# Other places in VectorE's queue for a recurrence's products and updates, an earlier residual load, and later sums of an input norm

## The chip, the cores and the metric

The program runs on one core of a Trainium2 chip. The core has five engines with a queue each: TensorE (PE in the profile, its weight loads PEld), VectorE (DVE), ScalarE (ACT), GpSimd (POOL) and SyncE (SP), which issues all the DMA transfers here. Each queue is worked off in order; semaphores hold an instruction back until the data it needs are there. The metric is the device time of one execution in microseconds (us); lower is better.

## The reference

One inference step of a two-layer decoder: layer 0 is a gated DeltaNet, layer 1 an RWKV-7 time mixing; each is a pre-norm sub-layer with a residual add, and a final norm follows. All data are float32. There are 1104 token columns: 64 sample tokens (8 sequences of 8), 16 meta tokens and 1024 prompt tokens.

```python
def rwkv_mixer(xn, S0, shift_prev, ...):
    xx = xprev - xn
    xs = xn[None] + xx[None] * mu[:, None, None, :]
    rkvz = jnp.einsum('sbtd,sde->sbte', xs[:4], w_rkvz)      # r, k, v, z
    w = -jax.nn.softplus(-(w0 + jnp.tanh(xs[4] @ w1) @ w2)) - 0.5
    a = jax.nn.sigmoid(a0 + (xs[5] @ a1) @ a2)
    kk = l2norm((k * k_k).reshape(B, T, H, N))
    k = k * (1.0 + (a - 1.0) * k_a)
    decay = jnp.exp(-jnp.exp(w))
    def step(S, inp):                                        # per token
        S = (S * d_t[:, :, None, :]
             + jnp.einsum('bhvk,bhk->bhv', S, -kk_t)[..., None] * b_t[:, :, None, :]
             + v_t[..., None] * k_t[:, :, None, :])
        return S, jnp.einsum('bhvk,bhk->bhv', S, r_t)
    ...
    y = (y - mean) * lax.rsqrt(var + GN_EPS) * lnx_w + lnx_b # per head
    y = y + jnp.sum(r_h * k_h * r_k, -1, keepdims=True) * v_h # the bonus
    y = y.reshape(B, T, D) * jax.nn.silu(z)
    return y @ w_o, S, xn[:, -1]

x = x + gdn_mixer(rmsnorm(x, norm_w[0]));  x = x + rwkv_mixer(rmsnorm(x, norm_w[1]))
y = rmsnorm(x, final_norm_w)
```

Outputs are the normed rows of prompt and sample, and the states of both layers.

## The kernel before

Activations lie feature-major: a tile has 128 features on the partitions and columns of tokens. The columns are worked in three thirds (`SEGS`: 384, 384 and 336 columns). Dense products keep float32 precision with three passes over split operands: a high part rounded to fp32r (made by ScalarE, instructions at L139: whi, yh, prh) and the remainder (GpSimd or VectorE, L143: wlo, yl, prl).

*Between the layers* (`gdn_out_norm`, L1200): for each third, eight output tiles of the DeltaNet's output projection are computed and added to the residual xb (L1196). After the eighth, `rwkv_norm` (L1246) squares the third on ScalarE, adds the squares on VectorE (rsum, L1260), sums over partitions with matmuls (frss), takes the root, spreads it with further matmuls against a diagonal dg (frb) and scales xb (L1275). The scaled input feeds the low-rank products (dlora). This stretch is not ordered by hand: a planner lists the instructions, and the order of the code gives their priority.

*Projections* (`projections`, L2394): the r, v and z products, ordered by hand in gaps between output tiles. In the same gaps 24 items are prepared (an item is a third times one of eight pairs of heads; `system_steps`, L1567): VectorE forms kk and al from k, a and the decay, TensorE the 64x64 systems (fL), and GpSimd inverts them step by step (L690, L692).

*The recurrence* (`wave`, L2531): rounds tau from -2 to 52. Each item starts at round T = 2n and takes six rounds, one per chunk of 64 columns, so that three items are under way at a time; the state is kept per pair of heads. A round has phases 0 to 3 (and 1.5). In phase 0 `step_solve` makes X from the state (ScalarE, L1891), in phase 1 `step_inner` solves (rA from X and rTT), then `step_state` updates the state (VectorE rS, L1920). Everything else is put into a plan with a round, a phase and a priority, and issued phase by phase in order of priority:

```python
        put = lambda tau, ph, f, prio: plan.setdefault((tau, ph), []).append((prio, f))

        def emit(*at):
            for _, f in sorted(plan.pop(at, []), key=lambda x: x[0]):
                f()
```

So the order in every engine's queue, SyncE's included, is the order of the plan. The steps that matter here, for an item at T:

- loads at T-5 and T-4 (cs, r, k2, al, v, kp);
- `reads` (L1738: r times decay, the two-input product AR) at T-3 and `pair` (L1742: pr, the bonus product of r, k and r_k), then `halves` (prh on ScalarE, prl on GpSimd);
- `bonus` (L1748) at T-2: matmuls fbonus with prh and prl, and rbv on VectorE; `scores` (G) in phase 1 of T-2 and T-1; `keys` (fBT) at T-1;
- `stats` of the chunk's output in phase 2 of each of its rounds (L1828, L1829);
- `rwkv_finish` (L1922) from T+5 to T+8: root of the variance (GpSimd's power, then three VectorE steps), normalised y (GpSimd, L1944), transposition dyT, t (L1952), the gated output lz (L1954), its split yh, yl (L1959). Items 22 and 23 have plans of their own;
- for the eight items of the first third, the sample sequences: `rwkv_sample_read` loads the states sn, transposes them (dsn) into Sb and reads them (drsr); `rwkv_sample_write` spreads the updates by sequence (ue), multiplies (drsw), adds to Sb (L2006) and decays it (L2007), transposes back (dsbT), copies (sso) and stores with four DMAs.

Filler matmuls run in phases 2 and 3 (`fill`, priorities 2.5 and 1): first the rest of z, then the output projection (`project_out`, L2021: tiles zo, added to the residual x2 at L2041), whose weights come as a stream (wraw, whi, wlo). `finish` (L2059) is the final norm of a third: transposes (fin), squares, times the weight (L2077), root, and the scaling by rows (L2092), which is GpSimd's in the first third. The PSUM tags of this part, with their buffers, are f (2), r (3), d, x and z (1 each), and a buffer is reused when its reader is done.

## Time and profile before

| | us |
|---|---|
| three runs | 2199.70, 2207.82 (median), 2214.87 |
| the profiled execution | 2200.14 |
| its span, first to last instruction | 2198.4 |
| TensorE busy in it | 2083.4 |
| VectorE, ScalarE, GpSimd busy | 1434.5, 1260.2, 1253.1 |

The clock column of a view is the TensorE clock granted, as a share of the full one. Over the whole span it was 0.98. In the rows of a view, an instruction is told by its engine, its line in the kernel, and output<-inputs by name; the first letter of a PSUM tile's name is its tag (drsw is a tile of tag d). "A <- B: total, times, longest" says that A waited for B. In a timeline, a bracket gives the idle time before an instruction and what ended it; a wait for several things is put down to the one that came last by the profile, and where the engine named had long been done it was another, often a DMA.

### The profile page before, as it was taken

To read this page: it belongs to the slowest core of one execution; us is meant where nothing else is said; L and a number is where in the kernel's file an instruction comes from. 1 tells how busy PE (TensorE), PEld (TensorE's weight loads), DVE (VectorE), ACT (ScalarE), POOL (GpSimd) and SP (SyncE) were. 2 spreads that over 40 slices of the span, in tenths; PEclk is the share of its full clock that TensorE was granted. 3 is DMA by queue.
4 is the path that set the end of the run, shared out by engine and by line. 5 is a ranking of instruction groups with operands and counts; after the bars stand their busy time and mean duration, and the time that the engine had idled before them with its cause. 6 is when DMAs were issued, how large, how long until landed. Compare 5 with 4: busy or idle time off the path is not lost. (4 is left out here: it accounts for less than half of the span.)

```text
span 2198.4 us, 56220 instructions
## 1 busy us (share of the span) xinstructions
PE 2083.4 (95%) x20958; PEld 1945.7 (89%) x20958; DVE 1434.5 (65%) x3644; ACT 1260.2 (57%) x3627; POOL 1253.1 (57%) x1896
## 2 busy tenths in 40 slices
PE   7999999999999999989998999999989988899997
PEld 6888989898999989978998999998879977798886
DVE  7868585767757585975434762767756346687765
ACT  6536565656655565645433474755655456677763
POOL 3428577685858585625240452228668736676873
PEclk9999999999999999999999999999999999999998
DMA  3324242424243332436244235587785666566543
GB/s 122 91 75 115 73 133 67 118 78 112 79 113 97 100 111 69 138 79 176 93 140 117 73 93 174 172 257 204 228 241 153 166 179 171 159 186 171 160 124 103
DMA packets 510763, 291.67 MB, mean 133 GB/s; under 512 B 240777, under 2 KB 495866, under 8 KB 510490
## 3 DMA queue, kind: packets, MB, share of 16 engines
q1 hardware_dynamic: 510490, 288.08, 46.6%
q8 instruction: 166, 2.72, 0.5%
q14 instruction: 107, 0.88, 0.1%
HBM read 195.66 MB, written 92.30 MB: 131 GB/s over the span
## 5 line engine op out<-in xcount | busy, mean ns | idle before, releaser
L143 POOL TENSOR_TENSOR wlo<-wraw,whi 128x512 fp32r<-128x512 f32 x190 | 250.7, 1320 | 229.5 <-ACT whi L139 200.4
L692 POOL TENSOR_TENSOR invT<-invT,invtmp 72x31 f32<-72x31 f32 (+36 forms) x341 | 213.4, 626 | 26.7
L634 DVE SCALAR_TENSOR_TENSOR cvy<-raw,cw,cvy 128x408 f32<-128x408 f32 (+2 forms) x288 | 200.4, 696 | 31.1 <-ACT cvy L115 27.0
L690 POOL TENSOR_TENSOR invtmp<-invA,invT 72x31 f32<-72x31 f32 (+36 forms) x341 | 203.8, 598 | 24.9 <-DMA invA<-rltd 5.1
L129 PE MATMUL d<-xc,whi 128*128 128x384 f32 (+1 forms) x640 | 175.7, 339 | 0.2 <-ACT ev L1434 0.2
L139 ACT CAST whi<-wraw 128x512 fp32r<-128x512 f32 x238 | 145.9, 615 | 34.5 <-DMA wraw<-in_rwkv_w_o 12.4
L129 PE MATMUL dv<-xc,whi 128*128 128x384 f32 (+1 forms) x480 | 154.2, 342 | 0.0
L129 PE MATMUL dz<-xc,whi 128*128 128x384 f32 (+1 forms) x480 | 152.2, 340 | 0.0
L115 ACT ACTIVATE w<-rA,nbp 128x128 f32<-128x128 f32 x144 | 45.1, 364 | 152.5 <-PE rA L129 150.1
L1944 POOL TENSOR_SCALAR y<-y,mv,grs 128x64 f32<-128x64 f32 x132 | 83.7, 651 | 66.5 <-DVE grs L164 53.3
L129 PEld LDWEIGHTS d<-xc,whi 128*128 128x128 f32 x640 | 117.0, 190 | 2.2 <-ACT ev L1434 0.5
L129 PE MATMUL d<-xc,wlo 128*128 128x384 f32 (+1 forms) x320 | 104.2, 335 | 2.1 <-DVE wlo L143 2.1
L160 POOL TENSOR_TENSOR ors<-ovar,cvals 128x6 f32<-128x6 f32 x24 | 34.1, 1422 | 125.0 <-DVE ovar L1122 125.0
L129 PE MATMUL dz<-xa,whi 128*128 128x384 f32 (+1 forms) x288 | 102.6, 356 | 0.5 <-DVE zg L906 0.5
L129 PE MATMUL dv<-xa,whi 128*128 128x384 f32 (+1 forms) x288 | 102.0, 354 | 0.0
L129 PE MATMUL d<-xa,whi 128*128 128x384 f32 (+1 forms) x336 | 95.9, 338 | 1.3 <-POOL xa L143 0.8
L129 PEld LDWEIGHTS dv<-xc,whi 128*128 128x128 f32 x480 | 89.0, 188 | 3.5 <-issue 3.0
L959 POOL TENSOR_SCALAR Sb<-Sb,eglb 128x128 f32<-128x128 f32 x128 | 88.6, 704 | 5.9 <-DVE usc L752 3.1
L129 PEld LDWEIGHTS dz<-xc,whi 128*128 128x128 f32 x480 | 89.9, 190 | 0.6 <-issue 0.2
L129 PE MATMUL d<-xh,whi 128*128 128x384 f32 (+1 forms) x256 | 82.1, 333 | 0.0
L129 PE MATMUL d<-xl,whi 128*128 128x384 f32 (+1 forms) x256 | 82.1, 334 | 0.0
L129 PE MATMUL d<-xh,wlo 128*128 128x384 f32 (+1 forms) x256 | 81.8, 333 | 0.0
(558 smaller groups left out, 7304.3 us busy)
## 6 DMA issues: line engine op xcount, KB each, us to landing
wraw<-in_gdn_w_in SPq DMA_DIRECT2D x96, 256.0 KB
wraw<-in_rwkv_w_rkvz SPq DMA_DIRECT2D x74, 256.0 KB
Sb<-in_state_gdn SPq DMA_DIRECT2D x64, 256.0 KB
wraw<-in_rwkv_w_o SPq DMA_DIRECT2D x48, 256.0 KB
E<-drow SPq DMA_DIRECT2D x24, 384.0 KB
attn<-drow SPq DMA_DIRECT2D x24, 384.0 KB
wraw<-in_gdn_w_out SPq DMA_DIRECT2D x36, 256.0 KB
out_s_gdn<-Sb SPq DMA_DIRECT2D x32, 256.0 KB
```

The lines of the kernel that those rows point to most:

```text
L115: return self.nc.scalar.activation(out, in_, func, bias=bias, scale=scale, **kw)
L129: self.nc.tensor.matmul(out, lhsT, rhs, start=start, stop=stop)
L139: nc.scalar.copy(hi, x)
L143: e.tensor_tensor(lo, x, hi.bitcast(F32), op=ALU.subtract)
L160: self.nc.gpsimd.tensor_tensor(y, x, half.broadcast_to(sh), op=ALU.pow)
L634: nc.vector.scalar_tensor_tensor(ys[s][:, 0:wd(s)], raws[s][:, k:k + wd(s)], cw[k], ys[s][:, 0:wd(s)], op0=ALU.mult, op1=ALU.add)
L690: v.tensor_tensor(tmp, A[:, j, j + 1:32].unsqueeze(2).broadcast_to([nb, n, m]), Tv[:, j, 0:m].unsqueeze(1).broadcast_to([nb, n, m]), op=AL ...
L692: v.tensor_tensor(Tv[:, j + 1:32, 0:m], Tv[:, j + 1:32, 0:m], tmp, op=ALU.subtract)
L959: nc.gpsimd.tensor_scalar(Sb[g][:, u], Sb[g][:, u], self.eglb[:, hv, 4 * g + u:4 * g + u + 1], None, op0=ALU.mult)
L1944: nc.gpsimd.tensor_scalar(y[:, q], y[:, q], mv[:, q, 0:1], P.rs[:, q:q + 1], op0=ALU.subtract, op1=ALU.mult)
```

## The change

Seven edits. (1) `rwkv_norm` becomes a generator: its squares follow the third as before, its sums come in the code after the second output tile of the next third, and the spreading after the third tile; the last third's follow at once. dg gets a third buffer. (2) Two memsets per item in `system_steps` go from GpSimd to VectorE. (3) In the recurrence, `reads` and `pair` go to the head of phase 2 of round T-3 (priorities -1.5 and -1.2, from 3.5 and from phase 3), `halves` to 2.95 there. (4) The sample read's transposes go from phase 3 to phase 2 (2.9); the sample write's add goes to -0.5, its decay becomes a step of its own at 3, the transposes back go to 2.4, and the four stores follow in two pairs, in phase 3 and at the next round's start. (5) The gated output goes to -2 in phase 2, its split to 2.6; for items 22 and 23 the root's VectorE steps go from phase 0 to phase 2. (6) The first three tiles of the residual are loaded from round 14 + 16 s, phase 3, and the further ones one tile earlier than before. (7) The final norm's row scaling in the first third goes from GpSimd to VectorE, and the second third's norm steps from priority 2.45 to 2.55, behind the filler.

```diff
--- before.py
+++ after.py
@@ -1218,12 +1218,17 @@
                 elif s == 0:
                     self.load_w(src(ft), into=w)
                 self.add_out(s, self.dense(w, 128, oh, ol, s, bufs=4), xb[ft], self.x1T[ft])
+                if s and ft in (1, 2):
+                    next(norm, None)
                 if s == 2 and ft == 1:
                     lw = self.lora_weights(flat(xa)[:, 0:2048], flat(xa)[:, 2048:4096], pool)
             if s == 0:
                 for ft in (0, 1):
                     self.load_w(src(ft), into=res[ft])
-            self.rwkv_norm(s, xb, og, pool)
+            norm = self.rwkv_norm(s, xb, og, pool)
+            next(norm)
+        for _ in norm:
+            pass
         return lw
 
 
@@ -1248,7 +1253,6 @@
         nc, t = self.nc, self.t
         c0, n = SEGS[s]
 
-        ssp = self.ps("f", 2, "rss")
         sum_ = t(lp, [128, 384], "rsum", 1)
         if n < 384:
             nc.gpsimd.memset(sum_[:, n:384], 1.0)
@@ -1258,14 +1262,17 @@
                 self.act(f(sq), d, AF.Square)
             if k:
                 nc.vector.tensor_tensor(sum_[:, 0:n], sum_[:, 0:n], sq[:, 0:n], op=ALU.add)
+        yield
+        ssp = self.ps("f", 2, "rss")
         for q in range(3):
             self.mm(ssp[:, 16 * q:16 * q + 16], sum_[:, 128 * q:128 * q + 128], self.ones[:, 0:16])
         ms, rs = t(lp, [128, 3], "rms", 2), t(lp, [128, 3], "rrs", 2)
         nc.vector.tensor_scalar(ms, ssp[:, 0:48].rearrange("p (q j) -> p q j", j=16)[:, :, 0], 1.0 / D, RMS_EPS, op0=ALU.mult, op1=ALU.add)
         self.rsqrt(rs, ms, lp, "rr")
+        yield
         rb = self.ps("f", 2, "rb")
         for q in range(3):
-            dg = t(lp, [128, 128], "dg", 2)
+            dg = t(lp, [128, 128], "dg", 3)
             nc.vector.tensor_scalar(dg, self.ident, rs[:, q:q + 1], None, op0=ALU.mult)
             self.mm(rb[:, 128 * q:128 * q + 128], self.ones, dg)
         nw = self.pcol["norm_w"]
@@ -1574,9 +1581,9 @@
         kk, iD = t(pool, [128, 384], "skk", 3), cs
         al, sq = t(pool, [128, 384], "sal", 3), t(pool, [128, 384], "sqs", 3)
         self.act(al[:, 1:384], cs[:, 0:383], AF.Exp, scale=-self.DEC)
-        nc.gpsimd.memset(c6(al)[:, :, 0:1], 1.0)
+        nc.vector.memset(c6(al)[:, :, 0:1], 1.0)
         if Q.s == 0:
-            nc.gpsimd.memset(al[:, 0:64].rearrange("p (b r) -> p b r", r=8)[:, :, 0:1], 1.0)
+            nc.vector.memset(al[:, 0:64].rearrange("p (b r) -> p b r", r=8)[:, :, 0:1], 1.0)
         self.act(sq, k, AF.Square, scale=pc("rwkv_k_k"))
         nc.vector.scalar_tensor_tensor(kk, k, pc("rwkv_k_k"), a, op0=ALU.mult, op1=ALU.mult)
         nc.vector.scalar_tensor_tensor(al, k, pc("rwkv_k_k"), al, op0=ALU.mult, op1=ALU.mult)
@@ -1797,10 +1804,10 @@
         put(T - 4, 1, lambda: load("k2", "al"), 0)
         put(T - 4, 2, lambda: load("v", "kp"), 0)
         put(*((T - 4, 2) if n else (-3, 1)), exps, 2)
-        put(T - 3, 2, reads, 3.5)
+        put(T - 3, 2, reads, -1.5)
         put(T - 1 - (n < 3), 2 + (n < 3), lambda: load("tt"), 0)
-        put(T - 3, 3, pair, 6)
-        put(T - 3, 3, halves, 6.1)
+        put(T - 3, 2, pair, -1.2)
+        put(T - 3, 2, halves, 2.95)
         put(T - 2, 1, lambda: scores(0), 2)
         put(T - 2, 2, values, 2.05)
         put(T - 2, 2, bonus, -1)
@@ -1811,15 +1818,17 @@
             read = self.rwkv_sample_read(P)
             go = lambda: next(read, None)
             put(*((T - 5, 3) if n > 1 else (-4, 3)), go, 5)
-            put(*((T - 3, 3) if n else (-2, 2)), go, 5.5)
+            put(*((T - 3, 2) if n else (-2, 2)), go, 2.9)
             put(T - 1, 1, go, 5)
             write = self.rwkv_sample_write(P)
             go2 = lambda: next(write, None)
             put(T, 3, go2, 1.2)
             put(T + 2, 1.5, go2, 4)
-            put(T + 2, 2, go2, 2)
-            put(T + 3, 2, go2, 5)
+            put(T + 2, 2, go2, -0.5)
+            put(T + 2, 2, go2, 3)
+            put(T + 3, 2, go2, 2.4)
             put(T + 3, 3, go2, 5)
+            put(T + 4, 0, go2, 5)
 
         def stats(ci):
             if ci == 0:
@@ -1832,13 +1841,13 @@
         if n < 22:
             f = self.rwkv_finish(P, 0, 6)
             e = T + 8 - (n > 19)
-            at = [(T + 5, 3, 0), (T + 6, 2, 0), (e, 1, 5.5), (e, 2, 3.4), (e, 3, 2.5)]
+            at = [(T + 5, 3, 0), (T + 6, 2, 0), (e, 1, 5.5), (e, 2, -2), (e, 2, 2.6)]
             plans = [(f, at + [(e, 3, 5)] * (s == 2))]
         elif n == 22:
-            plans = [(self.rwkv_finish(P, 0, 6), [(T + 5, 3, 0), (T + 6, 0, 4), (T + 6, 3, 0), (T + 7, 1, 5.5), (T + 7, 1, 5.55),
+            plans = [(self.rwkv_finish(P, 0, 6), [(T + 5, 3, 0), (T + 6, 2, 0.1), (T + 6, 3, 0), (T + 7, 1, 5.5), (T + 7, 1, 5.55),
                                                   (T + 7, 2, 0.6), (T + 7, 3, 5)])]
         else:
-            plans = [(self.rwkv_finish(P, 0, 4), [(T + 3, 3, 0.1), (T + 4, 0, 4.1), (T + 4, 3, 0.1), (T + 5, 1, 5.6), (T + 5, 1, 5.65),
+            plans = [(self.rwkv_finish(P, 0, 4), [(T + 3, 3, 0.1), (T + 4, 2, 0.2), (T + 4, 3, 0.1), (T + 5, 1, 5.6), (T + 5, 1, 5.65),
                                                   (T + 5, 2, 0.8)]),
                      (self.rwkv_finish(P, 4, 6), [(T + 6, 0, 2), (T + 6, 1, 2), (T + 6, 1, 2.1), (T + 6, 2, 2),
                                                   (T + 6, 2, 2.1), (T + 6, 3, 2), (T + 6, 4, 2)])]
@@ -2004,6 +2013,7 @@
         yield
         p8 = ps.rearrange("p (b k) -> p b k", k=64)
         nc.vector.tensor_tensor(P.Sb, P.Sb, p8, op=ALU.add)
+        yield
         nc.vector.tensor_tensor(P.Sb, P.Sb, DC[:, 6:14].unsqueeze(2).broadcast_to([128, 8, 64]), op=ALU.mult)
         yield
         op = self.ps("d", 1, "sbT")
@@ -2011,6 +2021,7 @@
             self.transpose(op[:, 128 * g:128 * g + 128], P.Sb[:, 2 * g:2 * g + 2, :].rearrange("p b k -> p (b k)"))
         so = t(self.fin, [128, 4, 2, 64], "sso", 2)
         nc.scalar.copy(so.rearrange("p g h k -> p (g h k)"), op)
+        yield
         st = self.o["s_rwkv"][0].rearrange("(g u) h v k -> u v g h k", u=2)
         for u in (0, 1):
             for h in (0, 1):
@@ -2024,7 +2035,7 @@
         c0, n = SEGS[s]
         for ft in range(8):
             if load:
-                for u in ((0, 1, 2) if ft == 0 else (ft + 2,)):
+                for u in (ft + 3,):
                     if u < 8:
                         nc.sync.dma_start(x2[:, u, 0:n], self.x1T[u][:, c0:c0 + n])
             if len(pairs) == 4 or ft % 2 == 0:
@@ -2089,7 +2100,7 @@
                 hs = slice(512 * h, 512 * h + 512)
                 v = y[h]
                 if s < 2:
-                    (nc.vector if s else nc.gpsimd).tensor_scalar(v[0:nr], v[0:nr], rs[0:nr], None, op0=ALU.mult)
+                    nc.vector.tensor_scalar(v[0:nr], v[0:nr], rs[0:nr], None, op0=ALU.mult)
                 else:
                     nc.vector.scalar_tensor_tensor(v[0:nr], ps[h][0:nr], rs[0:nr], self.fw[0:nr, hs], op0=ALU.mult, op1=ALU.mult)
                 if tt == 0:
@@ -2544,10 +2555,12 @@
             nc.sync.dma_start(self.fw, self.i["final_norm_w"].rearrange("(o d) -> o d", o=1).broadcast_to([128, D]))
 
         def out(s, a, b, *tags):
-            if a == 0:
-                X2[s] = t(self.fin2, [128, 8, 384], "x2", 2)
             return self.project_out(s, [P[8 * s + q].out for q in range(a, b)], range(a, b), tags, X2[s], a == 0)
 
+        def residual(s):
+            X2[s] = t(self.fin2, [128, 8, 384], "x2", 2)
+            for u in range(3):
+                nc.sync.dma_start(X2[s][:, u, 0:SEGS[s][1]], self.x1T[u][:, SEGS[s][0]:SEGS[s][0] + SEGS[s][1]])
         ZF = ("f", 2)
         jobs = [(gates, 4 * self.ZK + 1, -5, 14)]
         jobs += [(lambda s=s, a=a: out(s, a, a + 4, Z), 16, 15 + 16 * s + 2 * a, 23 + 16 * s + 2 * a) for s in (0, 1) for a in (0, 4)]
@@ -2589,9 +2602,11 @@
             for _ in range(k):
                 next(finals[s], None)
         finals = {}
+        for s in range(3):
+            put(14 + 16 * s, 3, lambda s=s: residual(s), 4)
         for steps, s in more:
             for u, k in steps.items():
-                put(*((int(u), 2, lambda s=s, k=k: norm(s, k), 2.45) if u == int(u) else (int(u), 3, lambda s=s, k=k: norm(s, k), 5)))
+                put(*((int(u), 2, lambda s=s, k=k: norm(s, k), 2.55 if s else 2.45) if u == int(u) else (int(u), 3, lambda s=s, k=k: norm(s, k), 5)))
 
         at = lambda tau: [(P[n], tau - 2 * n) for n in range(max(0, (tau - 4) // 2), min(24, tau // 2 + 1)) if 0 <= tau - 2 * n < 6]
         emit(-4, 3)
```

## The prediction

> **What bounds the kernel now.** I read the page first: one core, TensorE busy for 95% of the span.
>
> ```profile
> span 2198.4 us, 56220 instructions
> PE 2083.4 (95%) x20958; PEld 1945.7 (89%) x20958; DVE 1434.5 (65%) x3644; ACT 1260.2 (57%) x3627; POOL 1253.1 (57%) x1896
> ```
>
> So only 115 us of the span have no matmul in flight, and an edit that shortens other engines' work is worth what it takes out of those 115, or out of matmuls run at a lower granted clock. Second I read the busy time by stretch, cut where the work changes (columns: PE, weight loads, VectorE, ScalarE, GpSimd, then granted clock, DMA share, GB/s).
>
> ```profile
> 1185.00:1197.00 12.00, 7.78 (x34) 7.46 (x33) 5.83 (x18) 2.38 (x6) 0.85 (x1) 0.72 0.47 115
> 1236.00:1278.00 42.00, 39.69 (x244) 39.37 (x243) 37.65 (x68) 29.88 (x67) 25.03 (x26) 1.00 0.20 64
> 1405.00:1780.00 375.00, 354.26 (x3939) 335.84 (x3939) 230.18 (x392) 207.35 (x449) 234.45 (x414) 0.97 0.73 205
> 1824.00:1908.00 84.00, 73.33 (x1362) 62.43 (x1362) 55.47 (x179) 51.31 (x172) 52.97 (x64) 0.90 0.61 159
> 1908.00:2002.00 94.00, 92.58 (x1767) 85.27 (x1768) 75.23 (x234) 71.33 (x232) 66.87 (x84) 1.00 0.64 176
> 2002.00:2115.00 113.00, 104.55 (x1894) 95.72 (x1893) 80.82 (x268) 79.53 (x261) 84.26 (x101) 0.95 0.55 155
> 2115.00:2163.00 48.00, 38.84 (x494) 34.71 (x493) 32.15 (x104) 25.88 (x85) 31.29 (x34) 1.00 0.44 138
> ```
>
> The first two rows are the input norm; 1405 to 1780 is the projections, 1824 to 1908 the recurrence's rounds that carry sample updates, 1908 to 2002 plain rounds, 2002 to 2115 rounds with the first third's final norm, then the tail. Plain rounds are TensorE's (92.58 of 94): no reordering gains there. Idle time that a reordering can reach lies in the other rows: 4.2, 10.7, 8.5 and 9.2 us, with granted clocks of 0.72, 0.90 and 0.95.
>
> Third, who made TensorE wait: first in 1824 to 1908 (us in total, times, longest), then in 2002 to 2115.
>
> ```profile
> PE rA L133 <- ACT X L115: 6.1, 5, 2.6
> PE fG L129 <- DMA BK<-kpd: 2.0, 1, 2.0
> PE drsr L129 <- DVE Sb L2006: 1.6, 4, 0.4
> PE dsn L126 <- ACT sso L2013: 0.7, 2, 0.3
> ...
> PE fbonus L129 <- DMA wraw<-in_rwkv_w_o: 3.8, 2, 2.1
> PE rA L133 <- ACT X L115: 2.8, 5, 1.9
> PE fbonus L129 <- POOL prl L143: 1.7, 1, 1.7
> ```
>
> **The change part by part.** *Sample rounds.* The chain of waits explains the 6.1 us (start, us, what):
>
> ```profile
> 1860.10 0.56 DVE rbv L1753
> ...
> 1862.14 0.58 DVE Sb L2006
> 1862.75 0.69 DVE Sb L2007
> 1863.44 0.55 DVE lz L1954
> 1864.01 0.51 ACT yh L139
> 1864.55 0.32 ACT X L115
> 1864.91 0.80 PE rA L133 x10
> ```
>
> The gated output lz is last in VectorE's phase, behind both sample instructions; its cast yh stands in ScalarE's queue ahead of the next solve's X, and the solve waits. The change puts lz first (priority -2), the sample add at -0.5 and splits the multiply off to 3. lz then runs in the gap before rbv and X finds ScalarE free. The add, ahead of the statistics, frees the PSUM bank that drsr waits for. The transposes dsbT go ahead of the filler matmuls and dsn behind them, which covers the copy sso. The four stores of a sample move a phase later, so SyncE's queue no longer stands at them before the next loads. The product (reads, pair) moves to the head of odd rounds' phase, its halves from phase 3 to phase 2: on ScalarE and GpSimd they now go ahead of the second filler's casts, and on ScalarE ahead of the decayed state pre, which the next state update needs only after a whole solve. At the head, reads can meet its transfer fldr, issued a round before: behind it then wait pair, rbv, the sample add, the statistics and the next G. The view of VectorE's waits from 1890 to 2160 has no line for fldr, and reads moves forward by about the three statistics pairs only, so I cost it at nothing; without that cover it costs the transfer's delay once per item. Waits that go: 6.1 + 1.6 + 0.7 = 8.4 us; the 2.0 us for BK is a transfer and stays. I take seven eighths, 7.4.
>
> The rounds run at clock 0.90, so 73.33 x 0.10 = 7.3 us of matmul time are a slow clock, and no wait there is longer than 2.6 us; with the waits gone I take half of it back, 3.7. Together 11, bounds 4 (half the waits, no clock) and 15.7. A check from the sample matmuls' starts:
>
> ```profile
> 1812.28 1.03 PE L129 MATMUL drsw<-ue,BT 128*64 128x512 f32 x4
> 1825.57 1.03 PE L129 MATMUL drsw<-ue,BT 128*64 128x512 f32 x4
> ...
> 1906.96 1.03 PE L129 MATMUL drsw<-ue,BT 128*64 128x512 f32 x4
> ```
>
> Two rounds took 13.3 us before finished items had to be gated, and (1906.96 - 1825.57) / 5 = 16.3 after; 11 us less over five pairs is 14.1, between the two.
>
> The Trainium skill (TensorE: Matmul & The Clock Gate, Part 1) says the clock halves after an idle window of about 3.4 us; by that no wait here would cost clock, and the sum would be smaller by the clock terms (3.7 here, 2.6 below). The row with 0.90 differs, and I go by the row.
>
> *Rounds with the final norm.* GpSimd's queue there:
>
> ```profile
> 2069.74 3.51 POOL L2092 TENSOR_SCALAR Sb<-Sb,frs 128x512 f32<-128x512 f32 x2 [0.51 <-DVE frs L164]
> 2073.22 1.27 POOL L143 TENSOR_TENSOR wlo<-wraw,whi 128x512 fp32r<-128x512 f32 x1
> 2074.45 1.35 POOL L160 TENSOR_TENSOR grs<-va,cvals 128x6 f32<-128x6 f32 x1
> 2075.77 0.99 POOL L143 TENSOR_TENSOR prl<-pr,prh 128x384 fp32r<-128x384 f32 x1
> ```
>
> Two scalings of 3.51 us stand ahead of prl, which the bonus matmul waits for: the 3.8 (put down to a weight transfer that ended in between) and the 1.7. The change gives the six scalings to VectorE, at some 0.50 each:
>
> ```profile
> L2092 DVE TENSOR_SCALAR Sb<-Sb,frs x6: 482/501/1495, 2139.5 to 2160.9; 128x512 f32<-128x512 f32 x6
> L1738 DVE TENSOR_TENSOR AR<-fldr,fDp x24: 523/1048/1732, 1753.5 to 2100.3; 128x384 f32<-128x384 f32 x24
> ```
>
> That is 3 us more for VectorE, covered where it is busy 80.82 of 113; without that cover it costs the 3 us. The other 2.8 us hold one wait of 1.9 at the second third's first output tile:
>
> ```profile
> 2010.03 1.53 SPq L2029 DMA_DIRECT2D x<-x1T  x3
> ...
> 2012.78 0.56 DVE L2041 TENSOR_TENSOR x<-x,zo 128x384 f32<-128x384 f32 x1 [1.83 <-PE dyT L129]
> ```
>
> The add follows the issue of its residual by 2.7 us; pair and X stand behind it. The three loads now go out a round ahead, behind that round's own loads on SyncE, and pair no longer follows the add. Seven eighths of 8.3 is 7.3, half of 104.55 x 0.05 is 2.6; less a little for VectorE, 9. Bounds 4 and 13.5.
>
> *Input norm.*
>
> ```profile
> PE frss L129 <- DVE rsum L1260: 4.2, 1, 4.2
> ...
> PE dlora L129 <- ACT xh L139: 2.3, 1, 2.3
> ```
>
> The sums of the first third stand in TensorE's queue before VectorE has added the squares: 4.2 us, and 7.78 x 0.28 = 2.2 at the low clock. Two output tiles now go in front. But VectorE is busy 37.65 of 42 from 1236 on, where the stage ends with the 2.3; what TensorE gains can be waited out there. The third dg buffer works against that wait. I take 4; bounds -2.3 (the last wait doubles) and 8.7 (both go).
>
> *Projections.*
>
> ```profile
> PE fL L129 <- DVE skk L1584: 4.3, 3, 2.5
> ...
> DVE sal L1582 <- POOL sal L1577: 18.3, 10, 3.5
> ...
> L1577 POOL MEMSET sal<- x24: 100/108/111, 1413.9 to 1634.1; 128x6 f32 x24
> ```
>
> The memsets stand behind GpSimd's inversion steps and VectorE waits 18.3 us for them; three times TensorE waits in turn, 4.3. On VectorE the 32 cost some 0.11 each, 3.5 us in 375 with 230 busy, but there they wait for ScalarE's exponential with the other products queued behind. I take 2; bounds -3.5 and 4.3.
>
> *Tail.* Here, in 2115 to 2163:
>
> ```profile
> PE zo L129 <- DVE x L2041: 3.0, 1, 3.0
> ```
>
> The add stands behind the norm's instructions; they go behind the filler now (2.55), and the last items' root steps go behind the state updates. I take 2; bounds -2 (the norm, later, holds its PSUM banks) and 3.
>
> **The rivals.** *The clock comes back whole* where the waits go: the other 3.7 + 2.6 us, and all the waits (another 2), some 8 more than forecast: 2168. For it: plain rounds run at 1.00. Against: some waits always stay.
>
> *The sums don't move.* The input norm's stretch is ordered by a planner, not by hand; if it places the sums where it did, that part's 4 us stay: 2180. Later code order speaks against it.
>
> *The wait moves to VectorE.* Its queue is in order and no instruction has left it; ends of rounds may follow rbv and the add instead of lz. Then the sample rounds give 4, the norm rounds 7, the rest nothing: 11 us, 2193. For it: in the chain above VectorE is the bound for 3.9 us on end. Against: it is busy only 55.47 of 84.
>
> *Slower: blocked heads.* The product's first instruction takes 0.52 to 1.73 us, 1.05 at the median: up to 1.2 us more, beside GpSimd's work. Three such two-input instructions (reads, pair, lz) now lead a pair of rounds. In plain rounds VectorE has 18.8 of 94 us free, 2.7 in a pair of 13.3; from 0.9 us each on, the blocking exceeds that and lands on the next state updates. At 1.2 each, that is 3.6 - 2.7 = 0.9 a pair, over 24 items 22 us lost, and the gains of the recurrence go too; with 8 us gained elsewhere, 14 slower: 2218. The Trainium skill (SBUF — State Buffer, Who interferes with whom) has this as a rule: a VectorE instruction with two SBUF inputs and a GpSimd one that reads SBUF exclude each other. Against it: the same three are in the queue today and the plain rounds bear it.
>
> **How the numbers follow.** 11 + 9 + 4 + 2 + 2 = 28 us. The profiled execution took 2200.14 us, its span 2198.4; less 28 that is 2172. It lies 7.7 under the median of the three runs before (2207.82, from 2199.7 to 2214.87), near their lowest. With it as a fourth, the middle of the four is 2204, and all cases are counted from there: the forecast is 2176, its own range 2163 to 2188, from sums of 41 (the clock and norm terms near their upper bounds) and 16. Chances: forecast 0.46, whole clock 0.12, sums unmoved 0.12, VectorE 0.23, blocked heads 0.07. With the whole clock at 2168 and the VectorE case at 2193, 2158 to 2200 leaves out under 2 in 10. One per cent, about what a measurement of this kernel tells from no change, is 22 us: below 2186 lie most of the forecast, the whole clock and half of the sums' case, together 0.60; above 2230 only part of the blocked heads and what I have not seen, 0.07; the rest is 0.33.
>
> **What would show it.** Right: no wait of rA for X over 0.5 us between 1824 and 1908 and a clock above 0.95 there; sample matmuls some 14 us apart; no wait of fbonus in the norm rounds, with L2092 on VectorE alone; frss without its 4.2 us. Wrong: X late behind another cast, reads with a median well over 1.05, a longer wait of dlora, or a new wait for a transfer in the shorter rounds, where SyncE's issues come closer together.

## The result and the profile after

The changed kernel takes 2238.41 us (median of 4 runs, 2233.59 to 2244.25), the kernel before 2211.35 us on the same chip: ratio 1.0132, 95% interval 1.0085 to 1.018. It is slower by 1.3%, 27 us, where 28 us of gain were forecast; the range ended at 2200.

The page of the changed kernel has the same matmuls and a little less of the span filled by them:

```profile
span 2242.5 us, 56205 instructions
PE 2112.2 (94%) x20958; PEld 1968.8 (88%) x20958; DVE 1468.2 (65%) x3682; ACT 1258.2 (56%) x3627; POOL 1235.8 (55%) x1858
```

PE has 28.8 us more to do with the same 20958 matmuls, so part of the difference is a slower clock (0.967 granted over the span, 0.980 before). To see where, I cut both traces at the same instructions: the first square that the input norm writes into rsum, the first matmul of dlora, the first drsw, and reads (the product's first step) of items 9, 16 and 23, counted from 0. The numbers are us between them, of one profiled execution each; the last three columns are kernels of the experiments below.

| stretch | before | changed | halves back | casts as memsets | early gate in sample rounds |
|---|---|---|---|---|---|
| start to the input norm (same code in all) | 1155.3 | 1170.0 | 1163.7 | 1159.9 | 1158.8 |
| input norm, to dlora | 99.8 | 95.1 | 94.3 | 95.0 | 95.1 |
| projections, to first drsw | 544.7 | 547.4 | 547.0 | 548.6 | 545.9 |
| sample rounds, to item 9 | 101.4 | 97.5 | 91.9 | 94.8 | 94.9 |
| plain rounds, items 9 to 16 | 94.4 | 113.0 | 94.5 | 92.6 | 94.5 |
| rounds with final norm, 16 to 23 | 104.7 | 119.4 | 107.1 | 92.9 | 104.8 |
| rest | 98.1 | 100.2 | 98.8 | 88.1 | 98.8 |

The first row is code that the change does not touch: it differs by 14.7 us between the two profiled executions, so these two spans are 44.1 us apart and the medians only 27. The loss of the change itself stands in two rows, 18.6 and 14.7 us, the plain rounds and those with the final norm. The plain rounds were TensorE's alone before. The busy time by stretch, items 3 to 9, 9 to 16 and 16 to 23, of the changed kernel and then of the kernel before:

```profile
1819.38:1909.95 90.57, 79.17 (x1538) 67.36 (x1537) 64.31 (x202) 59.53 (x197) 50.75 (x63) 0.96 0.67 173
1909.95:2022.96 113.01, 99.40 (x1768) 89.40 (x1767) 85.46 (x234) 70.38 (x234) 67.63 (x88) 0.94 0.52 140
2022.96:2142.33 119.37, 105.20 (x1785) 94.87 (x1784) 92.67 (x254) 73.02 (x246) 67.01 (x88) 0.90 0.53 146
```

```profile
1807.54:1901.19 93.65, 82.24 (x1536) 70.22 (x1535) 62.76 (x204) 59.80 (x197) 55.68 (x67) 0.91 0.63 163
1901.19:1995.63 94.44, 93.03 (x1772) 85.03 (x1771) 74.44 (x234) 71.88 (x233) 66.20 (x84) 1.00 0.61 169
1995.63:2100.31 104.68, 98.33 (x1789) 90.25 (x1788) 78.06 (x253) 75.65 (x248) 75.47 (x92) 0.97 0.60 167
```

In the plain row TensorE's busy time went from 93.03 to 99.40 us at a clock of 0.94 where it was 1.00, and its idle time from 1.4 to 13.6. TensorE's waits of the changed kernel in the same three stretches name one wait (us in total, times, longest):

```profile
PE fG L129 <- ACT BT L1787: 7.9, 10, 3.2
...
PE fG L129 <- ACT BT L1787: 13.2, 12, 1.9
...
PE fG L129 <- ACT BT L1787: 14.1, 14, 2.0
```

The wait of rA for X is gone, as forecast (6.1 us before; 0.4 in the first of these stretches), but fG now waits as much for the copies BT, there and in all rounds after. BT is a ScalarE copy out of a PSUM buffer of tag f; there are two of these, and the next fG, written into the same two, starts when the copies have freed them. ScalarE's own waits in the plain rounds, before and then changed:

```profile
ACT prh L139 <- DVE pr L1742: 5.0, 7, 0.9
```

```profile
ACT prh L139 <- DVE pr L1749: 19.1, 6, 3.6
```

One odd round of the changed kernel shows the whole chain (start, us, what; idle time before it in brackets), from VectorE, GpSimd, ScalarE and TensorE in turn:

```profile
1988.83 3.03 DVE L1745 TENSOR_TENSOR AR<-fldr,fDp 128x384 f32<-128x384 f32 x1
1991.89 0.62 DVE L1749 SCALAR_TENSOR_TENSOR pr<-AR,pcol,BK 128x384 f32<-128x384 f32 x1
...
1987.94 1.29 POOL L143 TENSOR_TENSOR wlo<-wraw,whi 128x512 fp32r<-128x512 f32 x1
1989.18 1.02 POOL L143 TENSOR_TENSOR yl<-lz,yh 128x384 fp32r<-128x384 f32 x1
1990.15 1.29 POOL L143 TENSOR_TENSOR wlo<-wraw,whi 128x512 fp32r<-128x512 f32 x1
...
1992.60 0.51 ACT L139 CAST prh<-pr 128x384 fp32r<-128x384 f32 x1 [3.49 <-DVE pr L1749]
1993.02 0.47 ACT L1787 COPY BT<-fBT 128x384 f32<-128x384 f32 x1
1993.39 0.82 ACT L115 ACTIVATE pre<-rS,DC 128x64 f32<-128x64 f32 x3
1994.12 0.46 ACT L1787 COPY BT<-fBT 128x384 f32<-128x384 f32 x1
1994.47 0.73 ACT L115 ACTIVATE X<-xX,rk 128x64 f32<-128x64 f32 x3
...
1993.54 0.43 PE L129 MATMUL fG<-AR,BK 64*64 64x128 f32 x2 [1.77 <-ACT BT L1787]
1994.63 1.55 PE L129 MATMUL fG<-AR,BK 64*64 64x128 f32 x22 [0.66 <-ACT BT L1787]
```

reads takes 3.03 us and ends 0.42 us after the last of three GpSimd casts. The cast prh stands in ScalarE's queue ahead of everything else of the round, waits 3.49 us for the product, and both copies BT, the decayed state pre and the solve's X stand behind it. Before, ScalarE had this order:

```profile
1956.52 0.48 ACT L1780 COPY BT<-fBT 128x384 f32<-128x384 f32 x1 [0.82 <-PE fBT L126]
1956.90 0.82 ACT L115 ACTIVATE pre<-rS,DC 128x64 f32<-128x64 f32 x3
1957.89 0.48 ACT L1780 COPY BT<-fBT 128x384 f32<-128x384 f32 x1 [0.17 <-PE fBT L126]
1959.18 0.51 ACT L139 CAST prh<-pr 128x384 fp32r<-128x384 f32 x1 [0.82 <-DVE pr L1742]
```

There a late product delayed only X, and little: in the plain rounds before, rA waited for X once, 1.3 us.

### The profile page after: what moved, and what is told of

It is laid out like the page before. It is cut to its first block, busy times and chain, and to the rows that moved or that the text cites. A ratio compares the mean times of both kernels' runs of the same rounds, so it can differ in the third digit from the quotient of the medians.

```text
span 2242.5 us, 56205 instructions
## 1 busy us (share of the span) xinstructions
PE 2112.2 (94%) x20958; PEld 1968.8 (88%) x20958; DVE 1468.2 (65%) x3682; ACT 1258.2 (56%) x3627; POOL 1235.8 (55%) x1858
## 4 chain that ended last, share of the span: by engine, by line
PE 62%; DVE 17%; ACT 6%; DMA 6%; POOL 3%; issue 3%; SPq 2%; DVEq 0%; POOLq 0%; ACTq 0%
PE d L129 13%; PE dv L129 7%; PE dz L129 7%; PE rA L129 6%; PE do L129 3%; PE dk L129 3%; PE rA L133 3%; DVE cvy L634 2%; PE zo L129 2%; PE fG L129 2%; DVE AR L1745 2%; PE dq L129 2%; PE xX L133 1%; DMA wraw<-in_gdn_w_out 1%; PE dlora L129 1%
## 5 line engine op out<-in xcount | busy, mean ns | idle before, releaser
L1953 POOL TENSOR_SCALAR y<-y,mv,grs 128x64 f32<-128x64 f32 x132 | 79.0, 618 | 107.9 <-DVE grs L164 107.9
L129 PE MATMUL fG<-AR,BK 64*64 64x128 f32 x1152 | 59.7, 310 | 40.6 <-ACT BT L1787 38.7
L129 PEld LDWEIGHTS fG<-AR,BK 64*64 64x64 f32 x1152 | 41.8, 152 | 49.6 <-ACT BT L1787 46.4
```

The lines of the kernel that those rows point to most:

```text
L129: self.nc.tensor.matmul(out, lhsT, rhs, start=start, stop=stop)
L1953: nc.gpsimd.tensor_scalar(y[:, q], y[:, q], mv[:, q, 0:1], P.rs[:, q:q + 1], op0=ALU.subtract, op1=ALU.mult)
```

## The experiments

Theory: reads is held up by GpSimd's casts, and prh, moved ahead of BT on ScalarE, hands the delay to TensorE. Two rivals: the loss arises in VectorE's queue behind reads (the rival with blocked heads, as the prediction priced it), or it comes from another part of the change (the later stores, the scalings on VectorE).

**The product's move is the loss.** First the changed kernel with only the product's move undone (the lines below), and the kernel before with only this move made (the same lines the other way round):

```
-        put(T - 3, 2, reads, -1.5)      +        put(T - 3, 2, reads, 3.5)
-        put(T - 3, 2, pair, -1.2)       +        put(T - 3, 3, pair, 6)
-        put(T - 3, 2, halves, 2.95)     +        put(T - 3, 3, halves, 6.1)
```

> The changed kernel with the product alone (reads, pair, halves) back at its old places; all other parts of the change stay. Theory: the product's move is the whole loss, so a plain pair of rounds is 13.1 to 13.5 us again (17 in the changed kernel), TensorE's waits for BT are under 1 us in a plain stretch of 90 us, and the time is about 2190 us, ratio to the kernel before 0.985 to 0.995 (from the input norm 5, the sample rounds 3 to 8, the final norm up to 9, the projections -3). Rival, that another part makes the plain rounds long (the later stores on SyncE, the scalings on VectorE): the pair stays at 16 us or more and the ratio at 1.005 or more.

> The kernel before with the product's move alone (reads -1.5, pair -1.2, halves 2.95 in phase 2). If the move is the loss by itself: reads at 3 us in plain rounds, a pair of 16 to 17, fG waiting for BT 1 to 2 us twice a pair, ratio 1.010 to 1.020. If it needs other parts of the change (the gated output earlier, so that its cast yl runs beside reads): reads as before at 1.0 to 1.7 us, and the ratio 0.998 to 1.005.

Product back: 2195.88 us against 2201.83, ratio 0.9962 (0.9942 to 0.9982); items 9 to 16 take 95.3 us, 13.6 a pair; both are a little above what was expected (0.995 and 13.5). Product alone: ratio 1.0158 (1.0131 to 1.0186), the stretch 112.5 us, reads at 2.73 us in four of its seven items. So the move is the loss by itself and needs nothing else of the change.

**Which half of the move.** The changed kernel with only the last of the three lines undone (it moves both casts, prh on ScalarE and prl on GpSimd):

```
-        put(T - 3, 2, halves, 2.95)     +        put(T - 3, 3, halves, 6.1)
```

> The changed kernel with only the halves (the casts prh and prl) back at phase 3; reads and pair stay at the head of VectorE's phase. Theory S, ScalarE's order: prh stands in ScalarE's queue ahead of the copies BT and the solve's X, waits there for the product, and TensorE's fG waits for BT; so here fG's waits for BT fall under 0.3 us each and a plain pair is 13.1 to 13.7 us although reads still takes up to 3 us; ratio 0.985 to 0.997. Theory V, VectorE's head: reads at 3 us delays the statistics, the residual add and the masks of the next G behind it; then the pair stays at 15 to 17 us, with TensorE waiting for VectorE in place of BT, and the ratio is 1.003 to 1.013.

Ratio 0.9984 (0.9959 to 1.001): nearly all of the 1.3% is gone, though the ratio lies just above the expected 0.997. The plain stretch, TensorE's wait for BT in it, and reads (least, median and longest ns):

```profile
1896.94:1991.41 94.47, 92.81 (x1768) 83.55 (x1767) 79.00 (x234) 71.40 (x234) 68.09 (x89) 1.00 0.64 176
...
PE fG L129 <- ACT BT L1787: 0.3, 1, 0.3
...
L1745 DVE TENSOR_TENSOR AR<-fldr,fDp x24: 539/1186/3671, 1758.6 to 2098.5; 128x384 f32<-128x384 f32 x24
```

reads still takes 2.6 to 3.1 us at items 11 to 16, and the rounds are back at 94.5 us: what stands behind reads on VectorE has room. TensorE's waits for BT fall from 13.2 us to 0.3, so it is ScalarE's order that turns a late product into an idle TensorE; prl, which moved with prh, stands in no wait of the plain rounds of the changed kernel.

**The wait or the cast itself.** The changed kernel with the two casts at their new places, made from the loaded r and not from the product (their outputs are other ones, so the time is that of a kernel that leaves the product out of the bonus):

```
-            self.split(P.pr, P.ph, P.pl, "act", "pool")
+            self.split(ld["r"], P.ph, P.pl, "act", "pool")
```

> The changed kernel, with the halves prh and prl cast from the loaded tile r and not from the product pr: the outputs are other ones, the casts stand at the same places of the queues and are as long, but wait for nothing that VectorE makes. If the loss is the wait (prh at the head of ScalarE's queue waits for a product that VectorE finishes late, with BT, pre and X behind it): fG's waits for BT fall under 0.3 us each, a plain pair is 13.1 to 13.7 us, the ratio 0.990 to 1.000 (the halves moved back gave 0.998). If the place alone is it (0.5 us more of cast ahead of the copies BT): a plain pair of 14 us or more, and a ratio over 1.003.

Ratio 1.0045 (1.0023 to 1.0066), between the two, and a pair of 14.0 us: by the marks set beforehand this falls just on the side of the place alone. But the edit had a side effect. The wait for BT is gone from the plain rounds, while reads now takes 4.1 to 4.3 us there: prl no longer waits for pr and joins the row of GpSimd's casts. TensorE's plain stretch and its waits:

```profile
1899.18:1997.48 98.30, 91.43 (x1768) 83.07 (x1767) 85.55 (x234) 71.47 (x234) 67.44 (x88) 1.00 0.60 162
...
PE fG L129 <- ACT X L115: 6.5, 5, 1.4
```

At 98.3 us, 14.7 of the 18.6 us are back even with a longer reads (in the rounds with the final norm, 112.2 us, half of the loss). The row names X, but the start times tell what fG follows: at items 11 to 16 its first matmul starts 0.10 us after reads has ended and 1.2 to 1.4 us after the last copy BT. In the changed kernel it starts 0.05 us after a copy BT and 1.7 us after reads. So in the changed kernel the wait of prh is the main part, and what is left here is the hold-up of reads itself, made longer by prl; the cast's own 0.5 us on ScalarE delays no fG here, since none starts right behind a copy BT.

**Why reads is long.** The changed kernel with reads and pair on one SBUF input each (both leave out a factor, so the outputs are other ones):

```
-            nc.vector.tensor_tensor(P.AR[:, :, 1, :], c6(ld["r"]), c6(P.Dp), op=ALU.mult)
+            nc.vector.tensor_scalar(P.AR[:, :, 1, :], c6(ld["r"]), pc("rwkv_r_k"), None, op0=ALU.mult)
```

> The changed kernel with reads and pair made of one SBUF input each: reads leaves out the decay (r times a column instead of r times fDp) and pair leaves out the factor k, so the outputs are other ones, with the same places in every queue. If the two-input form is what GpSimd's casts hold up, reads takes under 0.6 us beside the same casts (3.0 in the changed kernel), the waits of fG for BT fall under 0.5 us each and a plain pair is 13.1 to 13.8; ratio 0.985 to 0.997. If reads is long for another reason (its transfer, fDp, GpSimd's casts whatever the form), it stays at 2.5 to 3 us, the pair at 16 to 17 and the ratio at 1.01.

Ratio 1.0077 (1.0054 to 1.01). A miss: the one-input form takes 0.40 us alone and 2.8 to 2.9 beside the casts.

```profile
1953.73 2.84 DVE L1745 TENSOR_SCALAR AR<-fldr,pcol 128x384 f32<-128x384 f32 x1
```

The number of inputs does not settle it. The next run leaves VectorE alone and takes away GpSimd's reads: in the recurrence each low half that GpSimd makes is filled with zero (the low halves are left out):

```
+        if eng_lo == "pool" and self.wave_on:
+            e.memset(lo.bitcast(F32), 0.0)
+            return
         e.tensor_tensor(lo, x, hi.bitcast(F32), op=ALU.subtract)
```

> The changed kernel, with each low half that GpSimd makes in the recurrence (yl, wlo, prl) filled with zero by a GpSimd memset at the same place of its queue: the low halves are left out, so the outputs are less exact; GpSimd still writes those tiles but reads none for them. If reads is long because GpSimd's casts read SBUF while VectorE needs a second read of it: reads takes 0.5 to 0.7 us in the plain rounds (3.0 in the changed kernel), prh waits little, fG waits for BT under 0.3 us each, a plain pair 13.1 to 13.7, ratio 0.985 to 0.997. If any GpSimd work beside it holds reads up, or its transfer or fDp does: reads stays at 1.5 us or more and the pair at 15 or more.

Ratio 0.9869 (0.9844 to 0.9893), 2173.12 us. GpSimd and VectorE in an odd round, then reads over all items:

```profile
1911.78 0.52 POOL L144 MEMSET wlo<- 128x512 f32 x1
1912.24 0.41 POOL L144 MEMSET yl<- 128x384 f32 x1
1912.61 0.52 POOL L144 MEMSET wlo<- 128x512 f32 x1
...
1912.27 0.55 DVE L1750 TENSOR_TENSOR AR<-fldr,fDp 128x384 f32<-128x384 f32 x1
...
L1750 DVE TENSOR_TENSOR AR<-fldr,fDp x24: 539/548/685, 1757.7 to 2083.7; 128x384 f32<-128x384 f32 x24
```

With GpSimd writing the same tiles beside it but reading none, reads takes 0.55 us while two of the memsets run: it is what GpSimd reads, not its work as such, that holds it up. The Trainium skill (SBUF — State Buffer, Who interferes with whom) says that a VectorE instruction with two SBUF inputs excludes a GpSimd one that reads SBUF but not one that only writes, and that a one-input instruction in a two-port mode excludes it too; 0.55 us beside memsets and 3.03 beside casts agree. For the one-input form, 2.84 beside casts, no run here shows in which mode it ran. As a time, 2173 us is no estimate of what the change is worth without the hold-up: the memsets are also shorter than the casts (0.41 to 0.52 us against 1.0 to 1.3) and wait for nothing.

**The other parts.** All on the changed kernel with the product back, or on the kernel before. The gated output to its old place as well:

```
-            at = [..., (e, 2, -2), (e, 2, 2.6)]     +            at = [..., (e, 2, 3.4), (e, 3, 2.5)]
```

> The changed kernel with the product and the gated output lz (and its casts) at their old places. If the gated output's place is what sped up the sample rounds (X late behind yh and lz, 6 us), the waits of rA for X come back to 4 us or more between items 3 and 9, that stretch goes from 86.3 to 91 or more, and the ratio from 0.9962 to 0.998 or more; reads in plain rounds goes from 2.0 us back to 1.7. If the gain came from the sample updates' places instead, the stretch stays at 85 to 88 us and the ratio at 0.995 to 0.997.

Ratio 0.9976 (0.9958 to 0.9995). Items 3 to 9 take 94.7 us, against 86.3 with the early gate, and X is late again:

```profile
PE rA L133 <- ACT X L115: 7.5, 4, 2.5
```

So the gated output's place is worth 8.4 us of the sample rounds of these two profiles. In the time it shows as some 3 us (0.9976 against 0.9962), with intervals that overlap. The input norm's part alone, on the kernel before (the yields, the two output tiles ahead of the sums, three buffers dg):

> The kernel before with the input norm's part alone. In the profiles of the changed kernels the stretch from the sums frss to dlora is 58.5 us against 63 us without the part. If that gain stays to the end: 4 to 5 us, ratio 0.9975 to 0.9985, frss waiting 1.1 us and not 4.2. If the next stage gives it back: ratio 0.999 to 1.001, with dlora's or a later wait longer by as much.

Ratio 0.9956 (0.9939 to 0.9974). The norm takes 94.7 us, 5.1 less than before. The interval's 6 to 13 us is more than that, and above what was expected. From the input norm to the end this profile is 10.7 us shorter than that of the kernel before; of the 5.6 beyond the norm, 2.8 lie in the sample rounds and 2.5 in those with the final norm, which the edit does not touch. What makes these stays open. The memsets back on GpSimd, with the product back as well:

```
-        nc.vector.memset(c6(al)[:, :, 0:1], 1.0)     +        nc.gpsimd.memset(c6(al)[:, :, 0:1], 1.0)
```

> The changed kernel with the product at its old places and the memsets of sal back on GpSimd. If the memsets on VectorE pay (prediction: 2 us of the projections, bounds -3.5 and 4.3), this is 2 us slower than the kernel with the product back (2196 us, ratio 0.9962), with fL waiting for skk 4 us again and 1.6 us without: ratio 0.997 to 0.998. If they cost, 0.994 to 0.996. The stretch from dlora to the first drsw, 545 to 549 us in the five profiles so far, should move by less than 3 us.

Ratio 0.9959 (0.9938 to 0.998), which can't be told from 0.9962. The traces lean towards a loss of some 3 us: in the seven profiled kernels with the memsets on VectorE the projections take 546.3 to 549.1 us, mean 547.9, in the eight with them on GpSimd 538.2 to 550.6, mean 544.7; the two ranges overlap. The changed kernel's waits there:

```profile
PE d L129 <- ACT whi L139: 5.8, 1, 5.8
...
PE fL L129 <- DVE skk L1591: 1.6, 1, 1.6
```

fL's wait fell from 4.3 to 1.6 us as forecast, and one of 5.8 to 6.0 us for whi came in all seven (0 to 1.3 in the eight others).

The final norm's parts left out (scalings on GpSimd, loads and tail as before), on the kernel with product and memsets back:

> The kernel before with the input norm's part, the gated output and the sample updates at their new places and nothing else of the change: scalings on GpSimd, residual loads, tail and memsets as before. By the prediction the parts left out give the rounds with the final norm 9 us and the tail 2, so this would be 11 us slower than the kernel that has them (0.9959): 1.001, with fbonus waiting for prl 5 us again. Rival: they give nothing, because the scalings on VectorE stand behind a root step that GpSimd's casts hold up; then the ratio is 0.993 to 0.997 and the stretch from the 16th to the 23rd product 102 to 107 us.

Ratio 0.9939 (0.9915 to 0.9962), against 0.9959 with them: no gain of theirs shows. A reason is in the trace of the kernel with the product back: the root's first step, a product of 128x1, stands beside the casts wlo, yl and wlo, and fG waits (in this view "issue": nothing that the profile names; it starts 0.1 us after reads, which stands behind the scalings).

```profile
2043.09 2.26 DVE L162 TENSOR_TENSOR fn_t<-frs 128x1 f32<-128x1 f32 x1
...
PE fG L129 <- issue: 4.6, 2, 2.4
```

The scalings' own move lengthened that row of casts. On GpSimd they waited for the root, so the row ended before them: the step took 0.43 to 0.62 us in the kernel before, beside yl alone, and 0.77 to 1.05 here, with the gated output early. With the scalings on VectorE the next wlo follows yl at once: 1.66 to 1.89 us even with the gated output at its old place, 2.0 to 2.26 with it early. With the root and scalings a round later (rounds 36, 40, 44 at priority -0.8 instead of 35, 39, 43 at 2.45):

> The changed kernel with the product and the memsets at their old places, and the root and scalings of the first third's final norm a round later (rounds 36, 40, 44, ahead of the statistics) where GpSimd's casts yl and wlo do not stand beside them. Theory: in the kernel with the memsets back, the root's first step, a product of 128x1 with two SBUF inputs, takes 2.26 us beside those casts, three times, with the scalings and the product behind it, and TensorE's fG waits 2.4, 2.2 and 2.0 us; here the step takes under 0.3 us, the 6.6 us of waits go, the stretch from the 16th to the 23rd product falls from 106.6 to 100 to 103 us, ratio 0.993 to 0.9945. Rival: the block moves to the grouped normalisation of y on GpSimd, which stands in those rounds; then the stretch stays at 105 or more and the ratio at 0.995 to 0.997.

Ratio 0.9931 (0.9905 to 0.9957). That step takes 0.15 us, and the stretch from item 16 to 23 101.5 us:

```profile
2040.26 0.15 DVE L162 TENSOR_TENSOR fn_t<-frs 128x1 f32<-128x1 f32 x1
...
1989.93:2091.38 101.45, 94.47 (x1786) 86.38 (x1785) 82.38 (x255) 74.62 (x246) 67.07 (x87) 1.00 0.63 174
```

Last, what the parts suggest together: input norm, sample updates, and the gated output early only for items 0 to 5, and that with the later root on top:

```
+            at = [(T + 5, 3, 0), (T + 6, 2, 0), (e, 1, 5.5)] + ([(e, 2, -2), (e, 2, 2.6)] if n < 6 else [(e, 2, 3.4), (e, 3, 2.5)])
```

> As the kernel without the norm parts, and the gated output at its new place only for the six items whose gate falls in the rounds with sample updates; after that it is where the kernel before has it. The sample stretch (third to ninth product) should be 86 to 87 us as with the early gate everywhere (93.7 before, 94.7 with the gate back), the plain rounds 94.5 and the norm rounds 102 to 105, as before: 5 us of the input norm and 7 of the sample rounds, ratio 0.992 to 0.9945. If the early gate also helps later rounds, this is slower than the kernel with it everywhere, 0.996 or more.

> The kernel with the input norm's part and the gated output early in the sample rounds alone (0.9922), and on top of it the first third's scalings on VectorE with the root a round later, ahead of the statistics. If the two add: the stretch from the 16th to the 23rd product goes from 104.8 to 100 to 102 us, fbonus does not wait for prl there, and the ratio is 0.989 to 0.992. If not, because GpSimd's casts come later here and then meet the root or the product, the stretch stays at 104 us or more and the ratio at 0.992 to 0.995.

The first: 2189.16 us against 2205.93, ratio 0.9922 (0.9892 to 0.9953), faster than both kernels; its stretches are in the table. The second: 0.9948 (0.9926 to 0.997). Its rounds with the final norm take 102.5 us, 2.3 less than the first's 104.8, but no gain shows in the time: the two intervals overlap, and so do those of the four best kernels that leave nothing out (0.9922, 0.9931, 0.9939, 0.9948).

## Why the prediction was wrong

**The step that failed** is the product's move. The prediction put its cost on ScalarE as "on ScalarE ahead of the decayed state pre, which the next state update needs only after a whole solve", that is at nothing. Two copies BT and X also stand behind prh there, and fG needs the PSUM buffers of the copies at once. In its place the runs show this: prh waits 19.1 us for the product in the plain rounds, TensorE 13.2 us for BT behind it, and with the slower clock that follows the stretch is 18.6 us longer; over the whole kernel the move costs some 37 us (ratio 1.0132 against 0.9962 with the product back). The prediction also costed the head by its transfer alone, at nothing. That held (fldr was late once, by 0.9 us), but it left the hold-up by GpSimd's casts to a rival.

**Blocked heads** was that rival, with 7% and 2218 us. Its mechanism came, its sizes and its place did not. It bounded the hold-up by 1.2 us, from rows in which reads shared little more than one cast; the move by three statistics pairs put it ahead of a row of three, and in the plain rounds it takes some 2.5 us more than the 0.55 it takes alone. And it let the delay land on VectorE's 2.7 us of room per pair; the halves moved back show that this room holds it, and that the loss went through ScalarE's queue.

**Sample rounds**, 11 us: to item 9 they gained 3.9 in the changed kernel, where the wait for BT (7.9 us) took the place of X's, and 93.7 - 86.3 = 7.4 from item 3 to 9 with the product back. The reading of the chain (lz, yh, X) was right: with the gate back X waits 7.5 us again. The clock rose from 0.91 to 0.98 there. The sample matmuls came 15.4 us apart in the changed kernel and 14.7 with the product back, where 14.1 was forecast and 16.3 measured before.

**Rounds with the final norm**, 9 us: 14.7 lost in the changed kernel; 1.0 lost with the product back (105.7). fbonus no longer waits for prl, as forecast, and two scalings take 0.88 us on VectorE, under the 1.0 taken. In the changed kernel the loss is again the wait for BT (14.1 us). With the product back it is the root step ahead of the scalings, which was not in the sum: 2.0 to 2.26 us beside the casts that GpSimd runs on with once the scalings have left it. Where that step is moved away, 3.2 us of the 9 are gained.

**Input norm**, 4 us: 4.7 (99.8 to 95.1), with frss waiting 1.1 us and dlora not at all. Right.

**Projections**, 2 us: about 3 lost, inside the bounds of -3.5 and 4.3. fL's wait went and a longer one came. That the wait for whi comes from the memsets is read off fifteen traces; how is not shown.

**Tail**, 2 us: from item 23 on, 100.2 us against 98.1 in the changed kernel, and 92.6 with the product back; the 3.0 us that zo waited for the add fell only to 2.5, and no run separates this part.

**The signs.** X's wait and frss went as announced, and the clock of the sample rounds rose to 0.96. The signs announced for wrong came too: a median of reads "well over 1.05" (1.62), and X behind another cast, prh, where TensorE waited for BT ahead of it. No new wait for a transfer decided anything.

## What to carry to other kernels

When a step moves ahead in one engine's queue, list what its consumer's cast or copy now stands ahead of on the next engine. Here a product 2 us late cost the plain rounds nothing (94.5 us) until an instruction that waits for it was first in an in-order queue that TensorE lives from. Before placing a VectorE instruction, look at what GpSimd reads at that very time; even a 128x1 product was held up for a row of casts. Work taken off an engine also takes away the pause that it made there. And measure parts alone: here one line of the change cost more than the others gained.

## What the runs showed of the hardware

In these traces a waiting VectorE instruction mostly did not get in between GpSimd casts that stand back to back. Before, reads took 1.72 us through the end of one cast and a second one; in the changed kernel 3.03 through the end of one and two more (three times it got in after the second, 1.78 to 1.89); with the casts of r 4.1 to 4.3, with prl as a fourth. In all of these it ended 0.41 to 0.42 us after the last cast that it waited for.

The clock halved after waits far shorter than the slow stretch that followed. In the odd round shown above, TensorE's waits of 1.77 and 0.66 us are followed by this (stretches of 0.7 us, the granted clock third from the end):

```profile
1993.50:1994.20 0.70, 0.43 (x2) 0.19 (x2) 0.70 (x3) 0.70 (x4) 0.68 (x1) 1.00 1.03 328
1994.20:1994.90 0.70, 0.27 (x5) 0.28 (x9) 0.46 (x2) 0.70 (x5) 0.61 (x1) 0.61 0.95 272
1994.90:1995.60 0.70, 0.70 (x19) 0.70 (x18) 0.00 (x0) 0.30 (x2) 0.70 (x1) 0.50 0.87 242
...
1997.00:1997.70 0.70, 0.70 (x16) 0.58 (x14) 0.44 (x2) 0.00 (x0) 0.00 (x0) 0.50 1.13 288
1997.70:1998.40 0.70, 0.70 (x25) 0.70 (x22) 0.43 (x1) 0.35 (x2) 0.00 (x0) 0.95 0.69 159
```

Some 3.4 us at half clock, about 1.7 us of matmul time, follow 2.4 us of waits; with waits of at most 1.4 us (the casts of r) the plain rounds ran at 1.00. The clock record of the trace gives a sharper rule. In the plain rounds of the changed kernel half clock begins at 1960.2, 1977.3, 1994.4 and 2011.4 us, whole multiples of 3.41 us apart, and lasts 3.41 us each time; in the 3.41 us ahead of each, TensorE was idle for 2.15 to 2.24 us. In the plain rounds of six kernels (before, changed, product alone, halves back, casts of r, one input) each of the ten windows of such a grid with 1.9 us idle or more was followed by half clock, and none with 1.5 us or less; in other parts of the traces windows between 1 and 2 us went both ways. This is why the loss is larger than the waits: 12.2 of the 18.6 us are idle time, 6.4 are matmuls at half clock. The Trainium skill (TensorE: Matmul & The Clock Gate, Part 1) has half clock after an idle window of about 3.4 us; the length of the slow stretch agrees, the idle time before it was shorter here, 2.2 of 3.41 us. The forecast's choice to go by the row was right.

And the same code from the start to the input norm took between 1155.3 and 1171.7 us in fifteen profiled executions: single profiles of two kernels can't be compared by their spans here, only stretch by stretch.
